# Second-layer operand sums read back from normalized x in DRAM, and HGRN2 keys turned by way of the values' row

## The chip, the cores and the metric

The kernel runs on one core of one Trainium2 chip. Times are device microseconds (us) of one execution. The kernel before has a median of 1062.06 us over 3 runs (1061.89 to 1062.87).

TensorE (PE) multiplies matrices; its weight loads are listed apart (PEld). VectorE is DVE, ScalarE is ACT, GpSimd is POOL, SyncE is SP. DMAs are issued from the queues of SP (the `dma` helper's default) and of ACT.

## The reference

One inference step of a two-layer decoder trunk in fp32, on 1024 prompt tokens and 8 x 4 sample tokens, 1056 columns in all, with a model width of 1024. Both layers are: RMSNorm, one input projection, a mixer times silu(gate), one output projection, a residual add.

```
layer 0 (RG-LRU, width 1536):  u = norm(x) @ w_in;  causal conv, two block-diagonal gates,
                               linear recurrence h;  x = x + (h * silu(gate)) @ w_out
layer 1 (HGRN2, 8 heads of 128): q, f, v, gate = split(norm(x) @ w_in)
                               q = silu(q); g = lb + (1 - lb) * sigmoid(f); k = 1 - g
    per head, chunks of tokens:  out = (q * decay) @ S + masked(q k^T with decays) @ v
                               S_new = decay * S + (k * decay)^T @ v
                               y = rmsnorm_per_head(out) * gain * silu(gate);  x = x + y @ w_out
final RMSNorm.  Outputs: y, the recurrent states, the conv inputs, the HGRN2 states.
```

## The kernel before

**Products.** Every fp32 projection is three reduced-precision matmuls (`mm3`, L254 to L256): the operands are split into a high part (a ScalarE copy) and a low part (a subtraction on DVE or POOL, L337). x of both layers is held as such pairs, `xh` and `xl`, eight rows of 128 x 1056 each; there is no row of the normalized x itself, which `scaled_parts` leaves in a passing buffer.

**Planning.** Nothing is issued in source order. A `Flow` collects operations with engine, estimated time, the keys that they read and write, and for DMAs a size in KB. `plan` simulates a list schedule, `back` gives priorities from the end, `search` tries random changes of the first 60 us, and `run` then emits each engine's instructions in the order found. The products that feed the main work are chained in source order (`main=True`), so PE's order is nearly fixed; the order on DVE, ACT, POOL and SP is the planner's. Each layer has a Flow of its own. In the second one (`exact`) the planner has one DMA time line for each issuing queue, at 250 KB/us each. Every engine, SP's queue among them, works in the order in which it was given its instructions.

**Second layer, heads 2 to 7.** `seven` computes each pair of projections of a head by seven block products in place of eight. Numbered products 1, 2, 3 and 5 take quarters of x or sums of two quarters, 4, 6 and 7 take sums. The sums of the right side don't depend on the head. They are made once: `build` (tables `TB[2]`, `TB[3]`, `TB[4]`) and `build1` (product 5's, written over the upper half of `xh[0..3]`, `xl[0..3]`), in 8 pieces (j, x) of 264 columns each. A piece's sum is added up from the high and low parts by `add` (L1377, DVE), then split by `parted_sum`. Products alternate between `NM7 = 3` PSUM banks. `plus` (L1510, DVE) adds a product to what stands in SBUF; for the values (`b == 2`) its last adds write the row `VT`.

**Recurrence.** Between the products stand four bursts of small matmuls per head: `burst1` to `burst4`. Head h's levels 0/1, 2/4, 8/16 and 32/64 (L1069 and L1123: quadrant matmuls; `scale` prepares the next level on DVE, L1051, and ACT, L1054) go with the state work of head h-1. `burst2(h)` holds levels 2/4 of h and `states(h-1)`: the products of keys and values per 128 tokens (L1222), and those of the sample tokens with the loaded state `si` (L1231). `outs` and `gated` make the output rows `SG`, which `gated` writes to DRAM as `yd` for the first six heads.

**Turning keys and values.** `states` needs both with the tokens across the partitions. At the end of `burst4(h)`, `turned` does this for the values (row `VT`, into `vflat`) and for the keys (row `B2`, into `kflat`): DVE transposes 32x32 blocks (L1172), one DMA of 512 KB writes the row to DRAM, and four DMAs of 128 KB read it back into the same row, each into 32 partitions. In what arrives, one token block of 128 keys is four pieces of 32 apart in the row, so `states` uses 4 x 4 matmuls per bank, each with 32 columns of keys as weights. The keys' buffer `kt` is also `on`, the normalized output of the head before.

**The sample state.** `advance` (h, 1) updates `si`, writes it out (`ss_out`) and issues the load of the next head's state into the same buffer, still in `burst3`.

The steps that follow refer to these places: `turned` and the keys' five transfers, `kt<-kt` in the profile (L323 is the helper's issue); the state load, `si<-in_s_in_dram`; the output rows, `yd<-sg`; the values' adds, `sg<-mm,k` at L1510, since `VT` is a row with the tag `sg`; the sums, L1377.

Of the kernel before, what the change touches and what calls it, by code (L numbers as in the profile page):

```python
# [14 lines left out]
F32 = mybir.dt.float32  # L15
# [26 lines left out]
CH = 352  # L42
# [4 lines left out]
H = 8  # L47
# [4 lines left out]
class Flow:  # L52
# [52 lines left out]
    def plan(self, key, stop=None):  # L105
# [6 lines left out]
        locked = taken = 0.0  # L112
        dma = {"SP": 0.0, "ACT": 0.0}
# [4 lines left out]
        for _ in range(n):  # L118
# [20 lines left out]
            ends[i] = max(free[e], dma[r] if kb else 0.0)  # L139
# [83 lines left out]
def tile_trunk(ctx: ExitStack, tc: tile.TileContext, xT, prm, hc, w0, wg, wo0, w1, wo1, s_in,  # L223
# [55 lines left out]
    x1a = [nc.dram_tensor(f"x1a_{m}", (128, TOK), F32, kind="Internal").ap() for m in range(KD)]  # L279
    x1d = [nc.dram_tensor(f"x1_{m}", (128, TOK), F32, kind="Internal").ap() for m in range(KD)]  # L280
# [28 lines left out]
    with ExitStack() as l0:  # L309
# [12 lines left out]
        def dma(dst, src, r=(), w=(), prio=5, kb=180, q=Q):  # L322
            fl.add("SP" if q is Q else "ACT", 0.45, lambda: q.dma_start(dst, src), r, w, prio, kb * (1.0 if r else 0.75))  # L323
# [338 lines left out]
        def out_last(src):  # L662
# [42 lines left out]
            for c in range(NCH):  # L705
# [78 lines left out]
        def smalls1():  # L784
# [21 lines left out]
            ttv(lbc, lb, lc, ALU.add)  # L806

# [131 lines left out]
    with ExitStack() as l1:  # L939
# [24 lines left out]
        on = fixed("kt", [128, 8, 128], F32, p1)  # L964
# [5 lines left out]
        vt, kt = (o.rearrange("p (a n j) -> p n a j", a=4, n=8) for o in (vflat, kflat))  # L970
        VK, KK = ([(o, i) for i in range(4)] for o in ("vt", "kt"))
# [197 lines left out]
        def turned(h, row, rk, dst, key, keys):  # L1169

            d = turn[key, h % 2]
            dve(1024, lambda: V.transpose(dst, row[:, :1024].rearrange("p (n b i) -> p b n i", n=8, b=4)), rk, keys, 3, True)  # L1172
# [648 lines left out]
```

## Time and profile before

| | |
|---|---|
| median of 3 runs | 1062.06 us (1061.89 to 1062.87) |
| the profiled execution's own time | 1063.88 us |
| its span, first to last instruction | 1062.2 us |
| mean granted TensorE clock | 0.994 |
| PE busy / PEld busy | 1041.7 us / 1011.9 us |
| DVE / ACT / POOL busy | 828.8 / 573.5 / 516.6 us |
| DMA | 119.89 MB, mean 113 GB/s |

The profile is of one execution. Busy time of an engine is the union of its instructions. A wait in it names what released the waiting engine by the last semaphore event that the profile saw; where that engine had long been done, it was something else, often a DMA. "issue" is time in which an engine waited for nothing that the profile shows. In the DMA lists a size is that of one transfer, and the last number is the median time from its issue to its landing.

### The profile page before, as it was taken

How to read it: one execution, taken by the hardware profiler on the slowest of the kernel's cores; microseconds unless marked ns; L12 is line 12 of the kernel's file. 1: busy time of each engine (PE TensorE's matmuls, PEld its weight loads, DVE VectorE, ACT ScalarE, POOL GpSimd, SP SyncE). 2: the span in 40 equal slices, each digit the busy share in tenths (PEclk: the TensorE clock that was granted, in tenths of full speed). 3: DMA queues.
4: the chain of work that ended last, by engine and by line, in shares of the span. 5: the costliest groups of instructions: out<-in, count | busy, mean ns of one | idle time of the engine just before them, and what ended most of it. 6: DMA issues, size and time to landing. Idle time of an engine off the chain costs nothing.

```text
span 1062.2 us, 26195 instructions
## 1 busy us (share of the span) xinstructions
PE 1041.7 (98%) x10220; PEld 1011.9 (95%) x10220; DVE 828.8 (78%) x1626; ACT 573.5 (54%) x1308; POOL 516.6 (49%) x601
## 2 busy tenths in 40 slices
PE   9999999999999999999999998999999999999997
PEld 9999999999999999999999998999999999999986
DVE  7999995788888689265887898897969796995436
ACT  6568656877765865334353463635454454652324
POOL 3426443443534355544757544555555545552544
PEclk9999999999999999999999998999999999999998
DMA  9201112123751586431222114342524242586204
GB/s 294 69 20 53 57 48 71 48 69 94 234 173 51 162 276 191 142 122 41 81 61 90 44 58 128 135 99 79 144 74 141 84 141 83 167 253 188 85 1 164
DMA packets 81643, 119.89 MB, mean 113 GB/s; under 512 B 10480, under 2 KB 59632, under 8 KB 81520
## 3 DMA queue, kind: packets, MB, share of 16 engines
q1 hardware_dynamic: 72304, 102.87, 31.6%
q10 hardware_dynamic: 9216, 15.35, 5.0%
q8 instruction: 80, 1.31, 0.5%
q14 instruction: 43, 0.35, 0.1%
HBM read 79.44 MB, written 33.87 MB: 107 GB/s over the span
## 4 chain that ended last, share of the span: by engine, by line
PE 90%; DVE 4%; DMA 3%; POOL 1%; issue 1%; ACT 0%; ACTq 0%; POOLq 0%; SPq 0%; DVEq 0%
PE mm L254 25%; PE mm L255 25%; PE mm L256 25%; PE hg L1069 1%; PE hg L1222 1%; PE hg L581 1%; PE hg L1277 1%; PE hg L1279 1%; PE hg L254 1%; PE hg L256 1%; PE hg L255 1%; DMA wraw<-in_w_dram 1%; DMA R<-in_xT_dram 1%; PE hg L1252 1%; PE mm L1069 1%
## 5 line engine op out<-in xcount | busy, mean ns | idle before, releaser
L254 PE MATMUL mm<-xh,whi 128*128 128x352 f32 (+1 forms) x1143 | 359.4, 314 | 0.0
L255 PE MATMUL mm<-xl,whi 128*128 128x352 f32 (+1 forms) x1143 | 354.8, 310 | 0.7 <-DVE xl L879 0.5
L256 PE MATMUL mm<-xh,wlo 128*128 128x352 f32 (+1 forms) x1143 | 354.4, 310 | 0.0
L337 POOL TENSOR_TENSOR wlo<-wraw,whi 128x256 fp32r<-128x256 f32 (+3 forms) x184 | 192.2, 1060 | 213.2 <-ACT whi L392 101.8
L255 PEld LDWEIGHTS mm<-xl,whi 128*128 128x128 f32 x1143 | 215.5, 188 | 3.2 <-DVE xl L879 1.0
L254 PEld LDWEIGHTS mm<-xh,whi 128*128 128x128 f32 x1143 | 215.2, 188 | 2.1
L256 PEld LDWEIGHTS mm<-xh,wlo 128*128 128x128 f32 x1143 | 215.3, 188 | 0.0
L513 DVE SCALAR_TENSOR_TENSOR k<-xb,prm_sb,k 128x352 f32<-128x352 f32 (+2 forms) x144 | 89.0, 628 | 15.2 <-ACT k L510 12.1
L254 PE MATMUL mm<-t,whi 128*128 128x264 f32 (+1 forms) x306 | 89.4, 292 | 0.0
L255 PE MATMUL mm<-t,whi 128*128 128x264 f32 (+1 forms) x306 | 87.7, 286 | 0.0
L256 PE MATMUL mm<-t,wlo 128*128 128x264 f32 (+1 forms) x306 | 87.5, 286 | 0.0
L1510 DVE TENSOR_TENSOR k<-mm,k 128x264 f32<-128x264 f32 x144 | 60.1, 425 | 25.8 <-PE mm L256 24.8
L337 POOL TENSOR_TENSOR wlo<-R,whi 128x256 fp32r<-128x256 f32 x64 | 56.8, 906 | 35.6 <-ACT whi L1437 26.4
L596 POOL TENSOR_TENSOR k<-X 128x352 f32<-128x352 f32 x36 | 43.8, 1226 | 45.0 <-DVE R L597 33.4
L392 ACT CAST whi<-wraw 128x512 fp32r<-128x512 f32 (+2 forms) x83 | 46.2, 574 | 27.4 <-PE mm L255 12.8
L254 PEld LDWEIGHTS mm<-t,whi 128*128 128x128 f32 x306 | 57.5, 188 | 0.5
L256 PEld LDWEIGHTS mm<-t,wlo 128*128 128x128 f32 x306 | 57.6, 188 | 0.0
L255 PEld LDWEIGHTS mm<-t,whi 128*128 128x128 f32 x306 | 57.6, 188 | 0.0
L1437 ACT CAST whi<-wraw 128x512 fp32r<-128x512 f32 x52 | 31.9, 617 | 38.4 <-PE mm L255 21.0
L254 PE MATMUL mm<-yh,whi 128*128 128x352 f32 x153 | 49.9, 326 | 0.0
L255 PE MATMUL mm<-yl,whi 128*128 128x352 f32 x153 | 49.4, 323 | 0.0
L256 PE MATMUL mm<-yh,wlo 128*128 128x352 f32 x153 | 49.4, 323 | 0.0
(459 smaller groups left out, 2561.8 us busy)
## 6 DMA issues: line engine op xcount, KB each, us to landing
wraw<-in_w_dram SPq DMA_DIRECT2D x57, 256.0 KB, 3.1
wraw<-in_w_dram ACTq DMA_DIRECT2D x35, 256.0 KB, 3.9
wraw<-in_wo_dram SPq DMA_DIRECT2D x34, 192.0 KB, 2.5
si<-in_s_in_dram SPq DMA_DIRECT2D x8, 512.0 KB, 6.4
vt<-sg SPq DMA_DIRECT2D x8, 512.0 KB, 3.6
sg<-vt SPq DMA_DIRECT2D x32, 128.0 KB, 3.4
kt<-kt SPq DMA_DIRECT2D x8, 512.0 KB, 3.4
kt<-kt SPq DMA_DIRECT2D x32, 128.0 KB, 6.1
```

The lines of the kernel that those rows point to most:

```text
L254: T.matmul(out, wh, xh, start=first, stop=False)
L255: T.matmul(out, wh, xl, start=False, stop=False)
L256: T.matmul(out, wl, xh, start=False, stop=last)
L337: emit = lambda: e.tensor_tensor(b, x, a.bitcast(F32), op=ALU.subtract)
L392: act(m, lambda hi=hi, raw=raw, m=m: S.copy(hi[:, :m], raw[:, :m]), rk, (hk,), prio)
L513: dve(u, lambda src=src, dst=dst, sh=sh, k=k: V.scalar_tensor_tensor(dst, sh(src, k), pc("cw", 12 * k + m), dst, op0=ALU.mult, op1=ALU.add ...
L581: fl.add("PE", 0.62, lambda ps=ps, i=i, c=c: T.matmul(ps[:96, :CH], gs[:, i, :], ST[:96, chunk(c)], start=True, stop=True), (("gs",), *((" ...
L596: pool(CH, lambda x=x, a=a, b=b: G.tensor_tensor(x, a.bitcast(F32), b.bitcast(F32), op=ALU.add), (ak, bk), (xk,), 3)
L1069: T.matmul(ps[32 * j:32 * j + 32, n * w:n * w + w], B[:, o:o + 32], q(slice(o, o + 32)), start=True, stop=True, tile_position=(0, 32 * j))
L1222: T.matmul(ps[w, n * 128:(n + 1) * 128], kt[:, 4 * i + n, a], vt[:, 4 * i + n], start=True, stop=True, tile_position=(0, 32 * a))
L1437: act(512, lambda: S.copy(hi, raw), (rk,), (hk,), 2)
L1510: dve(QT, lambda: V.tensor_tensor(o[0], z[0], u[0], op=ALU.add), (z[1], u[1]), (o[1],), 0)
```

## The change

1. **Sums from normalized x.** In the first layer's last projection (`out_last`), each normalized chunk is also written to DRAM (`xnd`, 24 writes of 128 x 352). `build` reads four pieces of it per (j, x) and makes three sums with three adds; before, seven adds of high and low parts. `build1` reads two pieces (one into the space of the low part that it will write) and makes its sum with one add; before, three. `build1` takes x = 1 ahead of x = 0 and inherits the chunks that it really overlaps.
2. **Keys by way of the values' row.** After the block transposition and the write to DRAM, the keys are read back into `VT`, the row from which the values have just been transposed. Two ScalarE copies of 512 columns (`keys_turned`) bring them into `kt`, with the 128 keys of a token block side by side. `states` now uses one 128x128 weight per token block: 8 matmuls per head in place of 32. A bank's state products wait for its half of the keys alone. The next values can be written into `VT` only after both copies.
3. **State and output transfers behind the keys.** The load of `si` moves from `advance` to the end of `burst4` and is made to wait for the keys' write to DRAM (heads 1 to 7); the write of `yd` moves there too and waits for the second key copy.
4. **The planner's DMA model** for the second layer: one time line for both queues, a transfer's end at least 2.4 us + KB/600 after its issue, and loads counted at full size.
5. **First layer's order.** Three entries on DVE and one in `smalls1` that emit nothing are added to the first layer's plan.

```diff
-            if kb:
-                r = e if self.exact else "SP"
-                dma[r] = max(dma[r], t0 + 2.6) + kb / 250.0
-                end = dma[r] - 2.15 - kb / 250.0
+            if kb and self.exact:
+                dma = max(dma + kb / 250.0, t0 + 2.4 + kb / 600.0)
+                end = dma - 2.15 - kb / 250.0
+            elif kb:
+                dma = max(dma, t0 + 2.6) + kb / 250.0
+                end = dma - 2.15 - kb / 250.0
...
                     scaled_parts(c, m, x, xk, bc, bk, pc("g1", m), ("P",), G if m % 4 == 3 else V, 4)
+                    dma(xnd[m][:, chunk(c)], x, (xk,), (("xn", m, c),), 6)
...
                 act(CH, lambda: S.activation(o, ps[:, :CH], AF.Silu), (pk,), ok, 0)
+                dve(CH, lambda: None, (pk, *ok), ok, 0)
...
+        def turned(h, o, row, rk, dst, keys, via, back):
+
+            d = turn[o, h % 2]
             dve(1024, lambda: V.transpose(dst, row[:, :1024].rearrange("p (n b i) -> p b n i", n=8, b=4)), rk, keys, 3, True)
-            dma(d, dst, keys, ((key, "d", h % 2),), 3, 512)
-            back = d.rearrange("(a i) (b m) -> b i a m", a=4, b=4)
+            dma(d, dst, keys, ((o, "d", h % 2),), 3, 512)
+            src = d.rearrange("(a i) (b m) -> b i a m", a=4, b=4)
             for b in range(4):
-                dma(dst[32 * b:32 * b + 32].rearrange("p (a m) -> p a m", a=4), back[b], ((key, "d", h % 2),), (keys[b],), 3, 128)
+                dma(via[32 * b:32 * b + 32].rearrange("p (a m) -> p a m", a=4), src[b], ((o, "d", h % 2),), (back[b],), 3, 128)
+
+        def keys_turned(h):
+
+            vk, back = [("VT", c) for c in range(4)], [("turned", b) for b in range(4)]
+            for k in back:
+                inherit(k, vk)
+            turned(h, "kt", *brow(h, 0), kflat, two("kt"), VT[:, :1024], back)
+            for i in range(2):
+                w = slice(4 * i, 4 * i + 4)
+                act(512, lambda w=w: S.copy(kt[:, w, :].rearrange("p n (a j) -> p n a j", a=4),
+                                            VT[:, :1024].rearrange("p (a n j) -> p n a j", a=4, n=8)[:, w]), (*back, *vk), (("kt", i),), 2)
...
                     for n in range(4):
-                        for a in range(4):
-                            w = slice(32 * a, 32 * a + 32)
-                            T.matmul(ps[w, n * 128:(n + 1) * 128], kt[:, 4 * i + n, a], vt[:, 4 * i + n], start=True, stop=True,
-                                     tile_position=(0, 32 * a))
-
-                pe(1.05, emit, (*KK, *VK), (pk,))
+                        T.matmul(ps[:, n * 128:(n + 1) * 128], kt[:, 4 * i + n, :], vt[:, 4 * i + n], start=True, stop=True)
+
+                pe(0.98, emit, (("kt", i), *VK), (pk,))
...
                 dma(ss_out[h], si.rearrange("p b v -> p (b v)"), two("si"), (), 6, 512)
-                if h + 1 < H:
-                    dma(si.rearrange("p b v -> p (b v)"), s_in[h + 1], (), two("si"), 4, 512)
...
-            if h < H - 2:
-                dma(yd[h], SG[h], ykeys(h % 2, 0, TOK), (("yd", h),), 4, 528)
...
             if h < H:
-                turned(h, VT, [("VT", c) for c in range(4)], vflat, "vt", VK)
-                turned(h, *brow(h, 0), kflat, "kt", KK)
+                turned(h, "vt", VT, [("VT", c) for c in range(4)], vflat, VK, vflat, VK)
+                keys_turned(h)
+                k = (("kt", "d", h % 2),)
+            if 0 < h < H:
+                dma(si.rearrange("p b v -> p (b v)"), s_in[h], k, two("si"), 4, 512)
+            if 0 < h < H - 1:
+                dma(yd[h - 1], SG[h - 1], (*ykeys((h - 1) % 2, 0, TOK), ("kt", 1)), (("yd", h - 1),), 4, 528)
...
+                got = []
+                for m, q in ((j + 4, up), (j, up), (j, lo), (j + 4, lo)):
+                    t, tk = next(temps)
+                    dma(t, xnd[m][:, q], (), (tk,), 5, 132)
+                    got.append((t, tk))
+                (t, tk), (u, uk), (l, lk), (d, dk) = got
+                add(QT, t, t, u, ALU.subtract, (tk, uk), tk)
+                add(QT, l, l, t, ALU.add, (tk, lk), lk)
+                add(QT, d, d, l, ALU.subtract, (dk, lk), dk)
+                for n, o, k in ((3, t, tk), (2, l, lk), (4, d, dk)):
+                    parted_sum(n, j, x, TB[n, 0][:, j, lo], TB[n, 1][:, j, lo], o, k, G)
...
+                    h, l = xh[j][:, up], xl[j][:, up]
+                    u, uk = l.bitcast(F32), ("T", 1, 1, j, x)
+                    dma(t, xnd[j][:, lo], (), (tk,), 5, 132)
+                    dma(u, xnd[j][:, up], (), (uk,), 5, 132)
+                    add(QT, t, u, t, ALU.subtract, (uk, tk), tk)
+                    parted_sum(1, j, x, h, l, t, tk, V)
```

More of the change, by code (lines that the diff above doesn't have):

```diff
@@ L111, in plan @@
         free = dict(self.busy)
-        locked = taken = 0.0
-        dma = {"SP": 0.0, "ACT": 0.0}
+        dma = locked = taken = 0.0
         for i in range(n):
@@ L134, in plan @@
             free[e] = end = t0 + us
-            if kb:
-                r = e if self.exact else "SP"
-                dma[r] = max(dma[r], t0 + 2.6) + kb / 250.0
-                end = dma[r] - 2.15 - kb / 250.0
-            ends[i] = max(free[e], dma[r] if kb else 0.0)
+            if kb and self.exact:
[4 more added lines that the diff above has]
+                end = dma - 2.15 - kb / 250.0
+            ends[i] = max(free[e], dma if kb else 0.0)
             took[i] = us
@@ L279, in tile_trunk @@
     x1a = [nc.dram_tensor(f"x1a_{m}", (128, TOK), F32, kind="Internal").ap() for m in range(KD)]
+    xnd = [nc.dram_tensor(f"xn_{m}", (128, TOK), F32, kind="Internal").ap() for m in range(KD)]
     x1d = [nc.dram_tensor(f"x1_{m}", (128, TOK), F32, kind="Internal").ap() for m in range(KD)]
@@ L322, in dma @@
         def dma(dst, src, r=(), w=(), prio=5, kb=180, q=Q):
-            fl.add("SP" if q is Q else "ACT", 0.45, lambda: q.dma_start(dst, src), r, w, prio, kb * (1.0 if r else 0.75))
+            fl.add("SP" if q is Q else "ACT", 0.45, lambda: q.dma_start(dst, src), r, w, prio, kb * (1.0 if r or fl.exact else 0.75))
         def act(n, emit, r, w, prio=5, more=0.0):
@@ L806, in smalls1 @@
             ttv(lbc, lb, lc, ALU.add)
+            v(lambda: None)
         def masks():
@@ L1365, in build @@
-                for n, *steps in chain:
-                    if n == 3:
-                        (a, u, _), (b, v, _), *steps = steps
-                        add(QT, t, F(a[:, u]), F(b[:, v]), ALU.subtract, (k,), tk)
-                    for a, u, sign in steps:
-                        if sign == 0:
-                            add(QT, t, F(a[:, u]), t, ALU.subtract, (tk,), tk)
-                        else:
-                            add(QT, t, t, F(a[:, u]), ALU.add if sign > 0 else ALU.subtract, (tk, k), tk)
-                    parted_sum(n, j, x, TB[n, 0][:, j, q], TB[n, 1][:, j, q], t, tk, G)
+                got = []
```

32 lines of the change are left out of this document (10 added, 22 removed).

## Prediction

> **What bounds the kernel now.** I read the page first, then who TensorE (PE) waited for, then stretches and queues around each wait.
>
> ```profile
> span 1062.2 us, 26195 instructions
> ...
> PE 1041.7 (98%) x10220; PEld 1011.9 (95%) x10220; DVE 828.8 (78%) x1626; ACT 573.5 (54%) x1308; POOL 516.6 (49%) x601
> ...
> q8 instruction: 80, 1.31, 0.5%
> ```
> ```profile
> PE hg L1222 <- DVE R L1447: 3.6, 1, 3.6
> PE hg L1222 <- issue: 2.1, 2, 1.1
> PE hg L1069 <- ACT R L1054: 1.6, 1, 1.6
> PE mm L254 <- DVE sg L541: 1.1, 1, 1.1
> ...
> PE hg L1231 <- issue: 0.9, 1, 0.9
> PE mm L1231 <- issue: 0.7, 1, 0.7
> ```
>
> PE is the bound: outside its idle time no other engine can shorten the run, and the span leaves 1062.2 - 1041.7 = 20.5 us of idle. Two kinds of wait stand in the change's way: one of 3.6 us ahead of the state products (L1222), and 2.1 + 0.9 + 0.7 = 3.7 us at "issue" inside the same bursts, where no semaphore explains the idle time.
>
> The long wait costs more than itself (a row is a stretch, its length, busy time of PE, PEld, DVE, ACT, POOL, the granted clock, DMA share, GB/s):
>
> ```profile
> 644.50:647.50 3.00, 3.00 (x145) 2.82 (x143) 2.92 (x9) 2.14 (x6) 1.94 (x3) 1.00 1.07 340
> 647.50:649.60 2.10, 0.07 (x6) 0.00 (x0) 2.10 (x3) 0.07 (x1) 2.10 (x4) 1.00 0.92 135
> ...
> 651.20:656.40 5.20, 5.19 (x82) 4.72 (x83) 3.42 (x9) 0.64 (x2) 0.21 (x1) 0.50 0.02 3
> ```
>
> PE is idle from 647.5 to 651.2, the granted clock falls to 0.5 and stays there for the 5.2 us after it: 2.6 us of work lost. So this stall costs 3.6 + 2.6 = 6.2 us. The page "TensorE: Matmul & The Clock Gate" of the Trainium skill (What's actually happening) says the clock is halved after an idle window of about 3.4 us and returns after about 3.4 us of work. The trace agrees on the halving, but the slow part measured 5.2 us; with 3.4 us the stall would be estimated at 3.6 + 1.7 = 5.3 us. I go by the row.
>
> Who ended the wait? The profile names a DVE combine (L1447) which these products don't read. The queue shows the keys:
>
> ```profile
> 641.58 0.55 SPq L323 DMA_DIRECT2D si<-in_s_in_dram  x1
> 643.26 2.33 SPq L323 DMA_DIRECT2D kt<-kt  x4
> ```
> ```profile
> si<-in_s_in_dram SPq DMA_DIRECT2D x1, 512.0 KB, 7.8
> kt<-kt SPq DMA_DIRECT2D x1, 512.0 KB, 5.8
> kt<-kt SPq DMA_DIRECT2D x4, 128.0 KB, 6.1
> ```
>
> (The second fence: issues between 636 and 652, KB each, median us to landing.) The four read-backs are issued from 643.26 on over 2.3 us and take 6.1 us, so the last lands near 651, when PE starts again. Ahead of them in the queue stand the state load (si) and, before it, 528 KB of output rows (yd), in a stretch whose DMA share is 0.92 to 1.07. One head earlier, with neither beside it, the same five transfers took
>
> ```profile
> kt<-kt SPq DMA_DIRECT2D x1, 512.0 KB, 4.0
> kt<-kt SPq DMA_DIRECT2D x4, 128.0 KB, 3.1
> ```
>
> **Part 1: sums from normed x.** The chain of seven adds per (j, x) becomes three, and three become one in the sums for product 5: 8 x 7 + 8 x 3 = 80 adds become 32.
>
> ```profile
> 600.00:630.00 30.00, 10.41 (x18) 1.00 0.14 37
> sum 130.00, DVE 48.47; mean DVE 24.23
> ```
>
> (Stretches of L1377 alone.) At 48.47 / 80 = 0.61 us, 48 removed adds free 29 us of VectorE. Its own time is worth nothing while PE is busy. What counts is what stood behind it: the key transposition of the head that stalls.
>
> ```profile
> 634.66 1.23 DVE L1172 STREAM_TRANSPOSE kt<-sg 128x1024 f32<-128x1024 f32 x1
> ...
> 641.91 0.43 DVE L1510 TENSOR_TENSOR sg<-mm,k 128x264 f32<-128x264 f32 x1 [0.40 <-PE mm L256]
> ```
>
> Of the 18 adds in 600:630, at least 10 go: 10/18 x 10.4 = 5.8 us, so that transposition can end near 635.9 - 5.8 = 630.1.
> Added: 24 writes of 176 KB and 48 reads of 132 KB, 10.6 MB. In the stretch that takes them the DMA engines are at
>
> ```profile
> 440.00:640.00 200.00, 196.92 (x2094) 192.23 (x2093) 148.48 (x288) 83.66 (x202) 110.18 (x116) 1.00 0.23 73
> ```
>
> At 0.23 and 73 GB/s, 14.6 MB move in 200 us; 10.6 MB more makes the share about 0.40. SP gains 72 issues at 0.34 us, 24 us in 200. I take zero. If that cover is gone (a read waits for its buffer and holds SP's queue), the weights and V rows behind it come late; bounds 0 to the 3.6 us of the one wait that late rows caused here. Product 5 is the first to need the late sums; a late read-back would show as a wait there.
>
> **Part 2: keys by way of the values' row.** Removed: TensorE's 32 small matmuls per head (64 records, since fp32 shows two), replaced by 8 full-width ones. Added: two ScalarE copies of 128x512 per head.
>
> ```profile
> L1437 ACT CAST whi<-wraw 128x512 fp32r<-128x512 f32 x52 | 31.9, 617 | 38.4 <-PE mm L255 21.0 <-DVE wraw L1447 11.1 <-PE mm L256 3.7
> ```
>
> At 617 ns that is 1.2 us per head, 10 us on an engine 54% busy. The pace on PE:
>
> ```profile
> 606.82 0.39 PE L1279 MATMUL hg<-a,R 128*128 128x128 f32 x2
> 607.04 0.39 PE L1277 MATMUL hg<-sg,attn 128*128 128x128 f32 x2
> ...
> 707.26 0.73 PE L1069 MATMUL hg<-R,a 128*32 128x32 f32 x62
> ...
> 707.84 0.78 PE L1069 MATMUL hg<-R,sg 128*32 128x32 f32 x63
> 708.73 0.86 PE L1222 MATMUL hg<-sg,kt 128*32 128x128 f32 x24
> 710.69 1.30 PE L1222 MATMUL hg<-sg,kt 128*32 128x128 f32 x40 [1.10 <-issue]
> 711.80 0.62 PE L1231 MATMUL mm<-si,ab 128*32 128x128 f32 x16
> ```
>
> A full 128x128x128 fp32 matmul starts every 0.22 us: 8 x 0.22 = 1.76 us. Now the 64 records take 0.86 (708.73 to the break at 709.59) plus 1.11 (710.69 to 711.80) = 1.97 us, less the tail of the break. The difference is a tenth of a us per head either way: bounds -1.6 to +0.3 over eight heads, taken as 0.
>
> The "issue" gaps are the real gain of this part. 20440 PE and PEld instructions over 80 instruction transfers are 256 apiece. In this burst the two level products (L1069) are 128 matmuls with 128 weight loads inside 1.5 us, then 128 more instructions in 2 us, so two blocks are used up faster than one is fetched. The burst with levels 8 and 16 also has 256 quick instructions, but slow products follow it at once, and no issue wait is listed for it:
>
> ```profile
> 610.92 0.73 PE L1069 MATMUL mm<-R,sg 128*32 128x32 f32 x62
> ...
> 611.50 0.69 PE L1123 MATMUL mm<-R,a 128*16 128x16 f32 x62
> ```
>
> With 32 instructions in 1.8 us the changed burst looks like that one. I take -3.4 of the 3.7 us (a tenth left for a bad fall of a block's edge), bounds -3.7 and 0. The Trainium skill, "Runtime: NRT & Kernel Launch" (Instruction fetch mechanics), states that crossing a 16 KiB block costs a tail bump that is mostly hidden. If it is right here, the gaps have another cause and stay; that is the second rival.
>
> The added wait: the add that writes the next values (L1510, first at 641.91) must wait until both copies have read the row. Keys ready: 630.1 + 4.0 (write) + 2.3 (issues) + 3.1 to 6.1 (landing) + 1.2 (copies) = 640.7 to 643.7, against 641.91. PE has three banks here (NM7), so two more products run on before it lacks one. The next head shows their pace and its own margin:
>
> ```profile
> 689.97 1.81 SPq L323 DMA_DIRECT2D kt<-kt  x4
> ```
> ```profile
> kt<-kt SPq DMA_DIRECT2D x4, 128.0 KB, 7.8
> ```
> ```profile
> 701.65 0.42 DVE L1510 TENSOR_TENSOR k<-mm,k 128x264 f32<-128x264 f32 x1
> ...
> 703.14 0.43 DVE L1510 TENSOR_TENSOR sg<-mm,k 128x264 f32<-128x264 f32 x1
> ```
>
> Adds of successive products stand 703.14 - 701.65 = 1.49 us apart, so the cover is 3.0 us, and at most 1.8 us of lateness stalls nothing. In this next head even today's 7.8 us land the keys near 689.97 + 1.81 + 7.8 = 699.6 and copied by 700.8, ahead of 703.14.
>
> **Part 3: state load and output rows behind the keys.** The state load moves past four read-backs on SP, the outputs past the copies. si is due when L1231 starts, 647.5 + 1.8 = 649.3 in the stalled head without its stall. The keys' read-backs are issued by 630.1 + 4.0 + 2.3 = 636.4 there, so si need go no later than today's 641.58 and lands by 641.6 + 7.8 = 649.4: just in time, and I take zero, with rival 3 as the other end. In the next head it lands at 689.97 + 1.81 + 7.8 = 699.6, against 711.80.
>
> **Part 4: the first layer's plan.** The empty entries emit nothing; they can only alter the planned order. PE's first-layer waits (L254 1.1 us above) bound it: +-1.1, taken as 0, since nothing in the trace tells the sign. The wait at L1069 (1.6) ends with ScalarE's copy, not with the removed adds: 0, bound -1.6.
>
> **Sum.** -6.2 - 3.4 + 0 = -9.6 us. The profiled execution took 1063.88 us (span 1062.2), 1.8 over the median 1062.06; the sum is made on it, 1054.3, and carried to the median: 1052.5.
>
> **Rivals.**
> 1. *ScalarE held by the copies (slower).* ScalarE works in order. If a plan expects 3.1 us and the keys take what they can, weight casts and the copies out of PSUM stand behind the copy.
>
> ```profile
> DMA to landing us min/median/max: 2.6/5.8/8.9
> ```
>
> (Issue to landing of all transfers into or out of kt.) 8.9 - 3.1 = 5.8 us late, less 3.0 of cover, is 2.8 us in each of the six heads of the seven-product stage: +16.8 - 9.6 = +7.2, 1069.3. It decides from 3.0 us late and eats the whole gain at 3.0 + 9.6/6 = 4.6. For it: the two crowded heads above show 6.1 and 7.8. Against: si and yd, which made them so, go behind.
> 2. *The issue gaps stay*, since fewer instructions were not what they waited for: 1062.06 - 6.2 = 1055.9. For it: the profile names no cause. Against: every such gap lies in the one burst with 384 quick instructions.
> 3. *The state load takes the keys' place.* Issued at 645.6 after the read-backs as they lie now, it lands at 653.4, 4.1 us after 649.3; with the half clock that is the old stall again: 1062.06 - 3.4 = 1058.7.
> 4. *The change doesn't get the keys earlier.* Landing near 651, plus 1.2, the next values wait 10.3 us, less 3.0 of cover: 7.3 idle in place of 3.6, the slow clock as now, +3.7 - 3.4: 1062.4.
>
> **Chances.** Forecast 0.52 (its own range 1050 to 1055.5); rival 2 0.11; 3 0.08; 4 0.07; slower 0.22, from 1064.2 to 1069.3. Measurement tells about 0.2%, 2.1 us, from no change. So faster 0.52 + 0.11 + 0.08 = 0.71, same 0.07, slower 0.22. The range from 1050 to 1064.5 leaves out most of rival 1 and a little below.
>
> **What would show it.** Right: no PE wait at the state products, clock 1.00 throughout the middle, no issue lines at L1222 or L1231, 32 adds in the sums, 16 records of state products per head, copies of keys done before the values' add. Wrong: PE waits at L1231 on si; VectorE's values' add or ScalarE's queue waiting on "turned" rows; the issue lines still there with fewer instructions; a new wait at the first products of the second layer.

## The result and the profile after

The changed kernel takes 1049.09 us (median of 4 runs, 1048.66 to 1049.25) beside 1062.46 us (4 runs, 1061.89 to 1063.69) of the kernel before in the same series: a ratio of 0.9872, 95% interval 0.9855 to 0.9889. It is faster by 13.4 us. The forecast was 1052.5: its two terms came in nearly at their size, and most of the 3.4 us that it lacked came from where the operand rows lie in SBUF, which no step of the change sets.

The profiled execution took 1049.25 us. From its page:

```profile
span 1047.4 us, 25549 instructions
...
PE 1036.1 (99%) x9836; PEld 1006.4 (96%) x9836; DVE 805.7 (77%) x1578; ACT 579.9 (55%) x1324; POOL 524.1 (50%) x601
...
q8 instruction: 77, 1.26, 0.5%
```

PE's idle time is 1047.4 - 1036.1 = 11.3 us, 9.2 less than before. Its busy time is 5.6 us less: the half clock had stretched it by 2.6 us, the other 3 us were not foreseen. PE's waits of 0.2 us and more, all of them (who waited, for whom: us in all, times, longest):

```profile
PE mm L255 <- DVE sg L543: 1.2, 1, 1.2
PE hg L745 <- DVE ones L267: 1.0, 1, 1.0
PE hg L1700 <- DVE sg L1690: 0.8, 1, 0.8
PE mm L255 <- DVE k L1521: 0.6, 2, 0.4
PE hg L292 <- DVE xb L449: 0.3, 1, 0.3
PE hg L1075 <- DVE R L1087: 0.2, 1, 0.2
```

State products are now L1237 and L1245, the level product is L1075: neither of the first two waits, for keys or at "issue". The wait of 1.6 us at the level product, which ended at 540.09, is gone (the 0.2 us left at L1075 are those of another burst, at 565.8). A small wait is new, at the adds of L1521. Where the 1.6 us went, the burst of that product shows. Before, then after:

```profile
537.75 0.73 PE L1069 MATMUL hg<-R,a 128*32 128x32 f32 x62
...
540.09 0.76 PE L1069 MATMUL hg<-R,sg 128*32 128x32 f32 x64 [1.56 <-ACT R L1054]
```
```profile
534.51 0.73 PE L1075 MATMUL hg<-R,a 128*32 128x32 f32 x62
...
535.19 0.75 PE L1075 MATMUL hg<-R,sg 128*32 128x32 f32 x64
```

Before, PE waited inside the burst for ScalarE, which first made two weight casts (538.18, 1.14 us) and then the copy that the second product reads. After, the second product follows the first at once.

The crowded head, in the queues (start, duration, engine and line):

```profile
616.03 0.34 SPq L325 DMA_DIRECT2D kt<-kt  x1
619.05 1.74 SPq L325 DMA_DIRECT2D sg<-kt  x4
...
624.43 0.33 SPq L325 DMA_DIRECT2D si<-in_s_in_dram  x1
```
```profile
614.72 1.25 DVE L1178 STREAM_TRANSPOSE kt<-sg 128x1024 f32<-128x1024 f32 x1
...
634.97 0.43 DVE L1521 TENSOR_TENSOR sg<-mm,k 128x264 f32<-128x264 f32 x1
```
```profile
624.07 1.14 ACT L1192 COPY kt<-sg 128x512 f32<-128x512 f32 x2
```
```profile
640.40 2.02 PE L1237 MATMUL hg<-sg,kt 128*128 128x128 f32 x16
642.35 0.81 PE L1245 MATMUL mm<-si,ab 128*32 128x128 f32 x16
```
```profile
640.00:660.00 20.00, 20.00 (x332) 18.77 (x320) 13.37 (x35) 9.39 (x34) 10.17 (x14) 1.00 0.26 85
```

The keys are transposed at 614.72, where it was 634.66; the work on PE runs some 7 us earlier there (the first add into `VT` 641.91 - 634.97 = 6.9), so the transposition moved 13 us ahead of its users. Both copies are done at 625.2, 9.8 us ahead of the values' first add and 15 us ahead of the state products, and PE is busy at full clock from 640 to 660. Sixteen records of state products take 642.35 - 640.40 = 1.95 us, against 1.97 before.

To see where the time went, the same products were matched in the two traces, and the start after less the start before was followed through the run. Cumulated, in us (a stretch by the times of before):

| stretch of before | change of the shift | what lay there |
|---|---|---|
| to 68 | -0.6 | start |
| 68 to 532 | -2.6 | first layer: no wait went, a steady drift |
| 532 to 546 | -1.8 | the wait of 1.6 at the first level product |
| 579 to 594, 706 to 719, 758 to 770, 867 to 880 | -1.2, -0.7, -1.0, -1.2 | the "issue" gaps: 0.9, 1.1, 0.7 and 1.0 |
| 615 to 625 | -0.5 | a gap of 0.2 and the burst around it |
| 642 to 659 | -5.8 | the stall and its half clock |
| 816 to 828 | +0.7 | the new wait at the adds |
| all, at the last product | -15.2 | |

The profiled executions themselves lie 1063.88 - 1049.25 = 14.6 us apart. That of before was 1.4 us above its median, which is why this is more than the 13.4 of the medians.

The drift of the first layer is seen best as products done in a stretch in which PE never idles (length, busy time of PE, PEld, DVE, ACT, POOL, clock, DMA share, GB/s). Before, then after:

```profile
100.00:500.00 400.00, 400.00 (x2453) 394.51 (x2452) 303.80 (x505) 248.30 (x481) 184.29 (x202) 1.00 0.39 118
```
```profile
100.00:500.00 400.00, 400.00 (x2468) 394.51 (x2467) 305.95 (x511) 250.11 (x485) 185.50 (x200) 1.00 0.42 128
```

Both are busy for all of the 400 us at clock 1.00, yet 15 more products fit in, 15 x 400/2468 = 2.4 us. Starts of successive 352-column products lie 160.0 ns apart, where it was 161.1; 264-column ones 121.8 ns in both. A faster pace with no wait removed is what the experiments had to explain, beside the two named terms.

### The profile page after: what moved, and what is told of

Same layout as the page of the kernel before. It is cut to its first block, busy times and chain, and to the rows that moved or that the text cites. A ratio compares the mean times of both kernels' runs of the same rounds, so it can differ in the third digit from the quotient of the medians.

```text
span 1047.4 us, 25549 instructions
## 1 busy us (share of the span) xinstructions
PE 1036.1 (99%) x9836; PEld 1006.4 (96%) x9836; DVE 805.7 (77%) x1578; ACT 579.9 (55%) x1324; POOL 524.1 (50%) x601
## 4 chain that ended last, share of the span: by engine, by line
PE 89%; DVE 7%; DMA 1%; issue 1%; POOL 1%; ACT 0%; POOLq 0%; ACTq 0%; DVEq 0%
PE mm L255 25%; PE mm L257 25%; PE mm L256 25%; PE hg L1075 1%; PE hg L583 1%; PE hg L1289 1%; PE hg L255 1%; PE hg L1291 1%; PE hg L256 1%; PE hg L257 1%; PE hg L1237 1%; DMA wraw<-in_w_dram 1%; DVE R L449 1%; PE mm L1075 1%; PE hg L1266 1%
## 5 line engine op out<-in xcount | busy, mean ns | idle before, releaser
L255 PE MATMUL mm<-xh,whi 128*128 128x352 f32 (+1 forms) x1143 | 358.9, 314 | 0.6 <-DVE k L1521 0.6
L339 POOL TENSOR_TENSOR wlo<-wraw,whi 128x256 fp32r<-128x256 f32 (+3 forms) x184 | 200.3, 1104 | 197.9 <-ACT whi L394 94.8
L255 PEld LDWEIGHTS mm<-xh,whi 128*128 128x128 f32 x1143 | 214.7, 188 | 2.9 <-DVE k L1521 1.0
L255 PE MATMUL mm<-t,whi 128*128 128x264 f32 (+1 forms) x306 | 89.4, 292 | 0.0
L339 POOL TENSOR_TENSOR wlo<-R,whi 128x256 fp32r<-128x256 f32 x64 | 59.0, 941 | 32.9 <-ACT whi L1448 14.7
L1521 DVE TENSOR_TENSOR k<-mm,k 128x264 f32<-128x264 f32 x144 | 59.9, 423 | 19.0 <-PE mm L257 18.3
L255 PEld LDWEIGHTS mm<-t,whi 128*128 128x128 f32 x306 | 57.5, 188 | 0.5
L255 PE MATMUL mm<-yh,whi 128*128 128x352 f32 x153 | 49.9, 326 | 0.0
```

Source lines behind the costliest of these rows:

```text
L255: T.matmul(out, wh, xh, start=first, stop=False)
L339: emit = lambda: e.tensor_tensor(b, x, a.bitcast(F32), op=ALU.subtract)
L1521: dve(QT, lambda: V.tensor_tensor(o[0], z[0], u[0], op=ALU.add), (z[1], u[1]), (o[1],), 0)
```

## The experiments

All times below are medians; a ratio is to the kernel before on the same chip in the same series. "Products" is the count of PE's records from 100 to 500 us, as in the rows above.

### Does a second execution of before show the same?

Edit: none, the kernel before as it is.

> The kernel before, unchanged, profiled a second time. Open: the changed kernel ran the first layer's middle 2.4 us faster with the same products (2468 matmuls against 2453 in the stretch from 100 to 500 us), which no step of the prediction has. Theory A (the pace of the wide products is a matter of the execution): this profile has a count other than 2453, by 5 or more, and its first burst of the second layer starts other than 524.8 us by 1 us or more. Theory B (the pace belongs to the order of the first layer): 2453 within 2, 524.8 within 0.5. In both the stall at the state products (3.6 us) and the issue gaps (3.7 us in all) are there again.

Measured: 1061.4 us in one run; 2454 products. Its waits, and the stretch after the stall:

```profile
PE hg L1222 <- DVE sg L1060: 2.1, 1, 2.1
PE hg L1222 <- issue: 1.9, 2, 1.2
PE hg L1069 <- ACT R L1054: 1.6, 1, 1.6
```
```profile
649.50:653.00 3.50, 3.07 (x60) 3.10 (x64) 3.36 (x9) 0.00 (x0) 0.15 (x1) 0.51 0.02 5
```

The pace of the first layer belongs to the program, not to the execution. The stall does vary: a wait of 2.1 us here, then 3.1 us of work at half clock, which loses half of that: 2.1 + 1.5 = 3.6 us, in place of 6.2. The sum made on one profile took a large instance of it. What ended the wait is the same in both traces: the semaphore of the keys' last read-back is signalled for the last time 0.35 us before the first state product, and PE's wait for this semaphore ends 0.03 us later. So it was the keys, and not the VectorE instruction that the view names.

### The parts one by one

**Quadrant products on the new keys.** The 8 full products of a head become 32 again, all else stays:

```diff
-                        T.matmul(ps[:, n * 128:(n + 1) * 128], kt[:, 4 * i + n, :], vt[:, 4 * i + n], start=True, stop=True)
+                        for a in range(4):
+                            w = slice(32 * a, 32 * a + 32)
+                            T.matmul(ps[w, n * 128:(n + 1) * 128], kt[:, 4 * i + n, w], vt[:, 4 * i + n], start=True, stop=True,
+                                     tile_position=(0, 32 * a))
```

> The changed kernel, but the state products are again 4 x 4 quadrant matmuls per bank (32 a head instead of 8), on the same keys; times given to the planner stay. Theory 1 (the issue gaps are the fetch of instruction blocks, used up faster than they come): the issue lines at the state products return, 2 to 4 us in all, and the time is 1051 to 1053 against 1049.1. Rival (the gaps had another cause, such as the late transfers, and went with it): no issue lines, 1049 within 1.

Measured: 1050.66 us (1050.32 to 1051.72), ratio 0.9881 (0.9865 to 0.9898). Its "issue" waits:

```profile
PE hg L1239 <- issue: 2.2, 2, 1.7
PE hg L1248 <- issue: 1.1, 1, 1.1
...
PE mm L1248 <- issue: 0.4, 1, 0.4
```

The gaps are back, 3.7 us in all as before, in the same bursts, with keys in place long before. So they come with the quick instructions, as the forecast said and against the rival that they stay. Where they fall, the traces show: count all of PE's recorded instructions (products, weight loads, semaphore waits) in order of start, and the product after a gap at "issue" of 0.25 us or more is number 193 or 194 modulo 256, in all 24 such gaps after the first 100 us, in the seven traces that have any. No wait for a semaphore of that length ends at these numbers. In 23 of the 24, a transfer of the instruction queue (q8) began 2.3 to 3.1 us before. So the gaps belong to the fetch of instructions in blocks of 256. "Runtime: NRT & Kernel Launch" of the Trainium skill (Instruction fetch mechanics) states blocks of 16 KiB, 256 instructions, which agrees with 2 x 9836 / 77 = 255 here, and says that the cost of crossing is mostly hidden, which this burst contradicts: 0.4 to 1.7 us a gap. The median rises by 1.6 us only, less than the 2 to 4 us expected. The profiled execution, with its 3.7 us of gaps, is the slowest of the four, and other waits are shorter in it (the one at L255 on sg 0.5 in place of 1.2). The gaps' net worth lies between 1.6 and 3.7 us.

**Without the four empty entries:**

```diff
-                dve(CH, lambda: None, (pk, *ok), ok, 0)
...
-            v(lambda: None)
```

> The changed kernel without the four empty entries in the first layer's plan. Theory 1 (they only alter the first layer's planned order; PE's waits there are 2.6 us in all): within 1.5 us of 1049.1, either way. Rival (the order of the first layer is worth the 3 us that the prediction lacks): 1051 to 1053, with the first burst of the second layer at 523.5 or later, against 521.7.

Measured: 1049.03 us (1048.93 to 1050.36), ratio 0.987 (0.9855 to 0.9885), 2467 products. They are worth nothing, and the pace isn't theirs.

**Old sums.** Part 1 undone (the diff's `build`, `build1` and `xnd` back as before), and the empty entries out:

```diff
-                    dma(xnd[m][:, chunk(c)], x, (xk,), (("xn", m, c),), 6)
...
-                for x in (1, 0):
+                for x in range(2):
...
```

> The changed kernel with the first part undone (sums from high and low parts with seven and three adds, no normalized x in DRAM) and without the empty entries, so the first layer is the kernel before's, order and all. Theory 1 (the sums matter by the VectorE work ahead of the keys' transposition and at the start of the second layer): the wait of 1.6 us ahead of the first levels (L1069) is back, the keys of the first crowded head are turned 5 us later than now but still land in time since the transfers are behind them; 1051 to 1053. Rival (the sums are the main gain): the stall at the state products is back with a halved clock, 1055 or more. For the first layer: if its pace belongs to its order, the first burst starts at 524.8 within 0.5; if it belongs to the execution, anywhere from 521 to 525.

Measured: 1054.5 us (1052.78 to 1055.04), ratio 0.9916 (0.9901 to 0.9931), 2453 products. No wait at the state products. The keys of the crowded head:

```profile
626.12 1.24 DVE L1174 STREAM_TRANSPOSE kt<-sg 128x1024 f32<-128x1024 f32 x1
628.79 1.25 DVE L1174 STREAM_TRANSPOSE sg<-sg 128x1024 f32<-128x1024 f32 x1
```

With all the old adds on VectorE, the keys are transposed ahead of the values and 8.5 us earlier than before, some 6 us of it ahead of PE's own shift: parts 2 to 4 do that by the order that the planner finds with them. The stall goes without part 1, but the pace stays at the old one. The 5.4 us that this run loses are more than the pace (3 to 4 us, below) and outside the range of either theory. The largest wait that remains is the one that part 2 adds, the next values waiting for the copies of the keys:

```profile
PE mm L255 <- DVE k L1522: 1.5, 3, 0.9
```
```profile
640.73 0.43 DVE L1522 TENSOR_TENSOR sg<-mm,k 128x264 f32<-128x264 f32 x1 [1.14 <-ACT kt L1188]
```

**State and output transfers at their old places** (part 3 undone):

```diff
+                if h + 1 < H:
+                    dma(si.rearrange("p b v -> p (b v)"), s_in[h + 1], (), two("si"), 4, 512)
...
+            if h < H - 2:
+                dma(yd[h], SG[h], ykeys(h % 2, 0, TOK), (("yd", h),), 4, 528)
...
-            if 0 < h < H:
-                dma(si.rearrange("p b v -> p (b v)"), s_in[h], k, two("si"), 4, 512)
-            if 0 < h < H - 1:
-                dma(yd[h - 1], SG[h - 1], (*ykeys((h - 1) % 2, 0, TOK), ("kt", 1)), (("yd", h - 1),), 4, 528)
```

> The changed kernel with its third part undone: the state load and the output rows are issued where the kernel before issues them, ahead of the keys. Theory 1 (crowding by these two made the keys late): the keys' read-backs take 6 to 8 us instead of 3 to 4 in the crowded heads, the values' adds come close to waiting, 1050 to 1053. Rival (the earlier transposition alone leaves room enough): within 0.8 of 1049.1.

Measured: 1049.01 us (1048.6 to 1049.42), ratio 0.9874 (0.9859 to 0.9888). With the keys early, part 3 is worth nothing. The queue shows why:

```profile
618.37 1.73 SPq L325 DMA_DIRECT2D sg<-kt  x4
620.51 0.36 SPq L325 DMA_DIRECT2D out_ss_out_dram<-si  x1
621.77 0.34 SPq L325 DMA_DIRECT2D yd<-sg  x1
623.76 0.33 SPq L325 DMA_DIRECT2D si<-in_s_in_dram  x1
```

Once the keys are early, the read-backs stand ahead of si and yd without being told to. The order of issue is that of the changed kernel, so crowding by the two had no trial in this run; the run of part 1 alone, below, has one.

**The old DMA model in the planner** (part 4 undone):

```diff
-            if kb and self.exact:
-                dma = max(dma + kb / 250.0, t0 + 2.4 + kb / 600.0)
...
+                dma[r] = max(dma[r], t0 + 2.6) + kb / 250.0
+                end = dma[r] - 2.15 - kb / 250.0
```

> The changed kernel planned with the DMA model of the kernel before (one time line for each queue, 250 KB/us each, loads at three quarters). Theory 1 (the order follows from the dependences; the model changes little): within 1.5 us of 1049.1, the wait of 1.6 us ahead of the first levels of the second layer may come back. Rival (the model is what gets the keys out in time): waits of 1 to 4 us at the values' adds or at the state products, 1052 or more.

Measured: 1049.26 us (1048.02 to 1050.32), ratio 0.9876 (0.9861 to 0.989), 2467 products. Worth nothing. Of the first wait of the second layer, 1.6 us before and none after, 0.6 us are left here, at the next level product (540.82).

**Part 1 alone**, on the kernel before. Edit: the lines of part 1 in the diff, none of the others.

> The kernel before with the first part alone (sums from normalized x). Theory 1 (VectorE's adds ahead of the keys' transposition made them late): the transposition comes some 6 us or more earlier, the stall at the state products is gone with its slow clock (6 us), the issue gaps stay (2.5 to 3.7 us), and the first layer is at the changed kernel's pace (2468 products in 100 to 500 us, 2.5 us): 1053 to 1055. Rival (the crowded queue makes the keys late whatever VectorE does): the stall stays at 1 us or more, 1057 to 1060.

Measured: 1053.12 us (1051.76 to 1053.39), ratio 0.991 (0.9895 to 0.9925), 2468 products.

```profile
PE hg L1224 <- issue: 2.4, 2, 1.6
PE hg L1233 <- issue: 1.6, 1, 1.6
PE hg L1125 <- DVE R L1053: 1.2, 1, 1.2
...
PE mm L1233 <- issue: 0.4, 1, 0.4
```
```profile
622.05 1.23 DVE L1174 STREAM_TRANSPOSE kt<-sg 128x1024 f32<-128x1024 f32 x1
```

The stall is gone with the keys at 622.05; the "issue" gaps stay, 4.4 us of them; 1.2 us of the first wait are left, at the next level product; and the faster pace is here. The output rows and the state load are still issued ahead of the keys' read-backs (624.62 and 624.99, the read-backs from 626.04), yet no product waits for the keys. So these two alone, ahead in the queue, don't make the stall.

**Part 2 alone**, on the kernel before: `turned`, `keys_turned` and the full-width state products of the diff.

> The kernel before with the second part alone (keys by way of the values' row, full-width state products). Theory 1 (late keys now hold up the next values): no issue gaps, but in the first crowded head the keys come after the values are due and PE stands 2 to 7 us there, with a slow clock: 1058 to 1062. Rival (the plan moves the transposition forward because the values now wait for it): no stall, 1053 to 1055. First layer as before, 2453 products in 100 to 500 us.

Measured: 1057.69 us (1056.57 to 1059.26), ratio 0.9952 (0.9935 to 0.9968), 2453 products.

```profile
PE mm L254 <- DVE k L1521: 1.8, 2, 1.6
PE mm L255 <- issue: 1.6, 1, 1.6
PE hg L1232 <- DMA sg<-vt: 1.3, 1, 1.3
```
```profile
620.00:660.00 40.00, 36.31 (x480) 35.10 (x479) 38.42 (x79) 19.05 (x46) 18.84 (x24) 1.00 0.42 122
```

No "issue" at the state products, though one of 1.6 at another place (947 us). The stall is split up: in the 40 us around it PE idles 40.00 - 36.31 = 3.7 us, now on adds and on the values' read-back, with VectorE busy 96% of that time; the longest single wait is 1.6 us, and the clock stays at 1.00. Neither theory fits: the keys hold up no add, the half clock doesn't come, and neither does the rival's gain. With part 1 added (the next run), PE's idle time from 600 to 660 us falls from 3.7 to 0.3 us, so here the 29 us that part 1 frees on VectorE are worth something.

**Parts 1 and 2 alone** (the three edits above that undo parts 3, 4 and 5, together).

> The first and second part together, without the third, fourth and fifth (transfers where they were, planner's old DMA model, no empty entries). Theory 1 (sums and keys carry the whole gain): within 1 us of 1049.1, no halved clock, no wait over 1.2 us in the middle. Rival (each of the other parts is covered for by the other one, and without both the keys come late): a wait at the values' adds or the state products, 1051 or more.

Measured: 1050.09 us (1049.44 to 1052.11), ratio 0.9887 (0.987 to 0.9904), 2468 products. The two parts carry the gain up to some 1 us, which the intervals don't tell from none; the trace has 0.6 us of "issue" at L255 and 0.6 at the level product after that of the first wait (541.88) that the whole change has not.

### Where does the first layer's pace come from?

The pace goes with part 1 (2467 or 2468 products with it, 2453 without), which edits the first layer only by 24 small transfers to DRAM. What the two programs differ in besides: the rows `xh` and `xl` and the rings of weights lie at other SBUF addresses, since the allocator places tiles by the planned program. One theory held that these addresses set the pace, the other that the added transfers or the order do. All kernels below pin addresses by cutting rows and rings out of one large tile.

**Before, with rows and rings at the addresses of after:**

```diff
-        for k in range(KD):
-            a = acts.tile([128, TOK], F32R, tag="P", name="xh")
-            b = acts.tile([128, TOK], F32R, tag="P", name="xl")
+        both = acts.tile([128, 16 * TOK], F32R, tag="P", bufs=1, name="xhl")
+        for i, j in zip([0, 15, 12, 9, 8, 5, 11, 4], [14, 13, 10, 7, 6, 3, 1, 2]):
+            a, b = both[:, i * TOK:i * TOK + TOK], both[:, j * TOK:j * TOK + TOK]
...
+            cycle([(o[:, 512 * at:512 * at + 512], (tag, i)) for i, at in enumerate(ats)])
```

> The kernel before with nothing changed but where its operands lie in SBUF: the 16 rows xh, xl and the rings of weights stand at the addresses that they have in the changed kernel (each group is one large tile, cut by hand). So far every run with the first layer of the kernel before shows 2453 or 2454 products in 100 to 500 us, every run with that of the changed kernel 2467 or 2468, and the two differ in the planned order and in these addresses. Theory A (addresses set the pace): 2467 or 2468, and 2 to 3 us off the time, 1059 to 1061 beside 1062. Theory B (the order of the first layer sets it): 2453 within 3, 1061 to 1063.

Measured: 1058.98 us (7 runs, 1055.98 to 1061.98), ratio 0.997 (0.9952 to 0.9988).

```profile
100.00:500.00 400.00, 400.00 (x2467) 394.51 (x2466) 304.79 (x509) 249.60 (x485) 186.98 (x199) 1.00 0.39 118
```

The old program, with its old DMA traffic (118 GB/s), takes the new pace.

**After, with rows and rings at the addresses of before:** the same edit on the changed kernel, rows at [10, 15, 6, 5, 12, 9, 0, 4] and [8, 14, 3, 2, 11, 7, 13, 1].

> The changed kernel with the same rows and rings at the addresses of the kernel before. Theory A (addresses set the pace): 2453 within 3 in 100 to 500 us, 1051 to 1052.5. Theory B (the order of the first layer sets it): 2467 or 2468, 1048.5 to 1049.8.

Measured: 1052.13 us (1051.52 to 1052.99), ratio 0.9906 (0.9889 to 0.9922).

```profile
100.00:500.00 400.00, 400.00 (x2453) 394.52 (x2452) 303.85 (x503) 248.34 (x480) 183.13 (x199) 1.00 0.41 126
```

And the reverse: the whole change at the old addresses has the old pace and costs 3.0 us more. The addresses set it.

**Rows or rings?** After, with the rows alone at before's addresses, and with the rings alone there:

> The changed kernel, the 16 rows xh and xl at the addresses of the kernel before, the weight rings at its own. Theory R (rows set the pace): 2453 within 3 products in 100 to 500 us, 1051 to 1053. Rival W (rings set it): 2467 or 2468, 1048.5 to 1050.

> The changed kernel, the weight rings at the addresses of the kernel before, the rows at its own. Theory R (rows): 2467 or 2468, 1048.5 to 1050. Rival W (rings): 2453 within 3, 1051 to 1053.

Measured: rows alone 1052.85 us (2 runs, 1052.66 to 1053.04), ratio 0.9906 (0.9881 to 0.993), 2454 products; rings alone 1049.05 us (2 runs, 1048.71 to 1049.4), ratio 0.987 (0.9845 to 0.9895), 2467 products. The two rows of products, rows alone and rings alone:

```profile
100.00:500.00 400.00, 400.00 (x2454) 394.51 (x2453) 303.25 (x503) 248.55 (x480) 184.24 (x198) 1.00 0.41 126
```
```profile
100.00:500.00 400.00, 400.00 (x2467) 394.51 (x2467) 305.51 (x511) 250.86 (x485) 185.53 (x198) 1.00 0.42 128
```

It is the rows. The second kernel also has its rows pinned, at the changed kernel's own addresses, and takes the changed kernel's time, so the pinning itself costs nothing.

**What in the rows?** A row is 4224 bytes, 128 more than a multiple of 256. In after all eight low rows lie an even number of rows from their high row, in before two of eight. So two placements of after's rows, each low row two rows behind its high row (0 modulo 256 bytes), and each directly behind it (128):

```diff
+        for i, j in zip([0, 4, 8, 12, 1, 5, 9, 13], [2, 6, 10, 14, 3, 7, 11, 15]):
```

> The changed kernel, each low row two rows (8448 bytes, 0 modulo 256) from its high row, and the eight rows of products 0 to 3 all alike modulo 256, those of 4 to 7 too. Theory M (the pace suffers when high and low row, or one step and the next, differ by 128 modulo 256): 2470 or more in 100 to 500 us, 1046.5 to 1049. Rival (no such rule): anything from 2450 to 2470.

```diff
+        for i, j in zip([0, 2, 4, 6, 8, 10, 12, 14], [1, 3, 5, 7, 9, 11, 13, 15]):
```

> The changed kernel, each low row directly behind its high row (4224 bytes, 128 modulo 256). Theory M: 2453 or fewer in 100 to 500 us, 1051 or more. Rival (no such rule): as likely 2468.

Measured, at 0: 1049.23 us (1048.83 to 1049.83), ratio 0.9872 (0.9852 to 0.9891); at 128: 1052.6 us (2 runs, 1052.15 to 1053.06), ratio 0.9903 (0.9878 to 0.9928). The two rows of products:

```profile
100.00:500.00 400.00, 400.00 (x2465) 394.51 (x2464) 304.61 (x510) 250.61 (x485) 187.35 (x198) 1.00 0.42 128
```
```profile
100.00:500.00 400.00, 400.00 (x2454) 394.51 (x2453) 303.47 (x503) 248.55 (x480) 183.68 (x198) 1.00 0.42 126
```

The distance of the pair goes with the pace in these four placements. But it is not proportional: with two even pairs of eight, before runs like none. And the further grouping in the first of the two, from which still more products were expected, brought none (2465). The starts in the traces go further. A chain of products runs through the eight pairs in turn, three products to a pair. In the whole chains from 100 to 500 us the three take, pair by pair, 483.0, 485.3, 481.6, 483.6, 484.9, 481.8, 485.9 and 482.6 ns in before, and 477.2 to 479.8 ns in after. With before's rows in the changed kernel the eight numbers of before come back within 0.1 ns. The two even pairs of before, the first and the sixth, don't run at after's pace; and where every pair is at 128, the later ones alternate between some 483 and 486 ns. So an even distance does not by itself give a pair the fast pace, and more than the address modulo 256 seems to count. That the rows' addresses are the cause is shown; the rule in them is open. No version was clearly faster than the changed kernel.

## Why the prediction was right or wrong

**The stall (-6.2): right in size, and wrong on what was needed.** It gave 5.8 us in the aligned traces, with clock 1.00 and no wait at the state products as named. The reading that the late keys ended the wait holds. The step "10 of 18 adds go, so the transposition ends 5.8 us earlier" was too narrow: it moved by 13 us ahead of its users, by 6 us where no add was removed, and each of parts 1 and 2 alone ends the half clock. So the lateness belonged to the planner's old order; why that order was late is not shown. It isn't that the values are transposed first, since they are in the changed kernel too (603.79). Also the stall of the profiled execution was a large one (3.6 us in the other trace), so the median's gain is nearer to 4 to 6.

**The "issue" gaps (-3.4): right.** All 3.7 us are gone, they come back with the small matmuls alone, and they stand at the edges of instruction blocks. The stretches that held them shrank by 1.2 + 0.7 + 1.0 + 1.2 = 4.1 us; what is above 3.7 is the bursts'.

**Part 2's own price (0): right.** 1.95 us per head against 1.97, copies of 0.62 us:

```profile
L1192 ACT COPY kt<-sg 128x512 f32<-128x512 f32 x16 | 9.2, 619 | 15.2 <-DMA sg<-kt 15.2
```

ScalarE does stand idle for 15.2 us in all before these copies, the mechanism of the slower rival, but in none of the heads does PE come to need what stands behind. That rival needed 3.0 us of lateness at the values' add; the crowded head had 9.8 us to spare.

**Part 1's transfers (0): right.** From 440 to 640 us the DMA share is 0.44, where 0.40 was estimated, and no late sum shows among PE's waits.

**Part 3 (0): right in sum, wrong as an argument.** Its worth is zero because the keys are early, not because si is just in time. In the working it stood as what kept the crowding from the keys; without it nothing changes.

**Part 4 and 5 (0): two terms of the sum were mis-sized, and here it failed.** "The wait at L1069 ends with ScalarE's copy: 0, bound -1.6": it went altogether, and the stretch shrank by 1.8. It is gone from that product in every changed plan; at the next level product 1.2 us come in its place with part 1 alone, 0.6 with the old model, 0.4 with part 2 alone and none with all, so the plan around the burst decides. "First layer's plan, +-1.1, taken as 0": the first layer gave 2.6 us, beyond its bound. The bound came from PE's waits, on the assumption that a PE without waits can't become faster. The runs showed another way: rows at other addresses, 1.1 ns less for each of the 352-column products, which are nearly all of the 2453 in 400 us: about 2.6, beside 2.4 by the count. Pinned to the old addresses, the changed kernel measured 1052.1, 1052.9 and, with another slow placement, 1052.6 us, next to the 1052.5 forecast. That they meet it so closely is luck: there the remaining errors cancel, a first wait not counted and a stall counted at its large instance.

**The rivals.** The copies didn't hold ScalarE to any effect; the gaps didn't stay; si didn't take the keys' place; the keys did get earlier. What is left as a new wait is 0.6 us at the adds of L1521, in two waits, the longer near 814 us.

**The range** took no account of a term that has no wait in the profile, and so its low end, 1050.0, lies above the result.

## What to carry to other kernels

A bound from waits covers only what waits can give back: where an engine is at 98%, compare also the pace inside its busy time, by counting instructions in a stretch without idle time, and know which addresses its operands have before crediting an edit. A stall in a planned kernel can be the accident of one plan: before crediting a part with its end, undo the part and see whether it returns. Bursts of many small matmuls can wait for their instructions, which shows as "issue" at the edge of a block and went here when they were merged into fewer large ones.

## What the runs showed of the hardware that was not expected

- The SBUF addresses of the rows that PE streams set its pace: 160.0 or 161.1 ns between 352-column products (264-column ones 121.8 in both), 3.0 to 3.8 us over this run. With the two rows of all eight pairs 0 modulo 256 bytes apart the fast pace was seen, with six or all of them at 128 the slow one; the rule is open.
- Bursts that use up instruction blocks of 256 within a few us leave PE idle for 0.3 to 1.7 us, always at the same place of the block.
- The half clock set in inside the wait, 2.1 us after the last product in the kernel before. With 647.50 to 649.60 at clock 1.00, the next stretch of its trace is

```profile
649.60:651.20 1.60, 0.00 (x0) 0.02 (x1) 1.56 (x4) 0.00 (x0) 0.74 (x2) 0.51 0.05 15
```

and in its second execution a wait of 2.1 us in all brought it, 1.7 us after the last product. In the kernel before with its rows and rings moved, the third trace with this stall, the wait of 2.1 us ended at 646.61 and the clock fell at 647.66, 1.05 us later. By the clock records, its pieces between two changes last 645.12, 6.83 and 399.36 us in the first trace, 645.12, 3.41 and 399.36 in the second: 189, 2 (or 1) and 117 times 3.413 us. So it changes on a fixed grid, and where a wait lies in the grid decides as well as its length: one of 1.7 us (quadrant products on the new keys) brought none. "TensorE: Matmul & The Clock Gate" of the Trainium skill (What's actually happening) names an idle window of about 3.4 us; in all three traces PE had been idle for 2.1 us at most when the clock fell. The slow time ran 6.8 us in the first (1.6 idle and 5.2 at work) and 3.4 us in the two others.
